# Rows of a down projection: from two raw blocks split in two parts to three raw blocks split product by product

## The chip, the core and the metric

The kernel runs on one core of one Trainium2 chip. Its time is the device time of one execution in microseconds (us). Before the change the median of 3 runs is 2338.86 us (2338.65 to 2340.06).

## What is computed

One layer of a decoder block on 1024 tokens of width 1024, all in float32: dilated attention in twelve heads and retention in four heads side by side, gated and projected, then a squared-ReLU MLP of width 4096. The change touches only the end of the MLP:

```python
xn2 = rmsnorm(x, norm2_g[l])
x = x + jnp.square(jax.nn.relu(xn2 @ w_up[l])) @ w_down[l]
```

Below, the result of the up projection after the squared ReLU is called h; it has 1024 rows of 4096 numbers. The down projection is `h @ w_down`.

## The kernel before

**Products of three terms.** TensorE multiplies float32 numbers in a rounded form, fp32r. So each factor is split into a high part (its rounding, written by ScalarE as a copy into an fp32r tile) and a low part (the residual, factor minus high part). A product is then three matmuls: high times high, high times low and low times high (`Pipe.group`, L218; its matmul is L223). Weights are split by `split` (L317): the copy at L318 on ScalarE, the residual at L319 on VectorE.

**Seven products instead of eight.** Both MLP projections use a Strassen-like scheme: a two-by-two block product is made from seven products N1 to N7 of sums of blocks. In the down projection a *unit* is one pair (c, t): c is one of 8 chunks of 512 inputs, t one of 4 groups of 128 rows of tokens, taken with the 128 rows 512 below. The 32 units run in the order of c, and of t within c. For one unit, each of the seven products takes one 128 x 256 block of rows (sums of parts of h, made during the up projection) and one 256 x 512 block of weights (sums of parts of w_down). A product is 6 matmuls: 2 blocks of 128 inputs, times three terms. A unit is 42 matmuls, the down projection 32 x 42 = 1344.

**Order on TensorE.** TensorE's order is that of the program. In the loop at the end, unit u runs N6, N5, N1 of unit u + 1, N7, N2 of unit u + 1, N3, N4. `down` (L1169) issues one product and reads its sum out of PSUM. N1 and N2 add up in bank a; N6, N7 and N4 in bank b, which ScalarE fills with minus N1 (L1187) before; N5 and N3 in bank d. After N2, N6, N5, N7, N3 and N4 the bank is added to Y in SBUF, by VectorE at L1195 (in chunk 0 some of these are plain copies by ScalarE, L1193). So N7 can start only when the sum after N6 has been read, N4 only after N7's has, N3 only after N5's has, and N2 only when ScalarE has copied N1's.

**Rows.** During the up projection `put_operand` (L1125) writes each sum of parts of h to the DRAM tensor `h_d`, laid out by chunk c and row group t, with the seven products of one unit side by side. `load_rows(u)` (L1142, DMA at L1146, issued on the SP queue) brings the block of unit u, 896 KB, into one of two raw places, which lie in the operand tile of N1 of the up projection (trace names xh and xl) once that is no longer needed. `split_rows` (L1148) splits it in two parts: the pair N1, N2 (one ScalarE copy of 512 columns at L1157, two GpSimd subtractions of 256 columns at L1160) and the other five (one copy of 1280 columns, five subtractions). The split pair goes to a pool of two, the split five to one of two places. `prepare(u)` (L1163), called at the start of the loop body, splits the five of unit u + 1, issues the load of unit u + 3 into the place that this frees, and splits the pair of unit u + 2.

**Weights.** The class `Weights` loads raw blocks of w_down (DMA at L176, SP queue too), forms the sums of blocks on VectorE (L153) and splits them. A weight buffer is free for the chunk after next when its product has run for t = 3 (`W.free`, L1199); the step that fills it is written at that place of the program. So a chunk has 7 splits and 4 sums for VectorE, written around its last unit and the first unit of the next chunk. N2's and N3's weights of odd chunks lie in two halves of one tile pair.

**Other adders to VectorE.** In chunks 2 to 5 every second unit adds one block of x to Y (L1253).

**Order on the other engines.** The order of the instructions on ScalarE, VectorE, GpSimd and the SP queue is chosen by a planner at build time, from the dependencies and from its own estimate of durations; at run time each of these engines takes its instructions strictly in that order, and one that waits holds up all behind it.

Of the kernel before, what the change touches and what calls it, by code (L numbers as in the profile page):

```python
# [10 lines left out]
F = mybir.dt.float32  # L11
R = mybir.dt.float32r
AF = mybir.ActivationFunctionType
OP = mybir.AluOpType
# [3 lines left out]
P = 128  # L18
# [188 lines left out]
class Pipe:  # L207
# [24 lines left out]
    def step(self, ps, terms, ends=None, first=True):  # L232
# [6 lines left out]
        def after(i):  # L239
# [11 lines left out]
           "N4": ("D", 0)}  # L251
DOWN = ("N1", "N2", "N6", "N5", "N7", "N3", "N4")
BANK = {"N1": "a", "N2": "a", "N6": "b", "N7": "b", "N4": "b", "N5": "d", "N3": "d"}
# [15 lines left out]
def hybrid_block(ctx: ExitStack, tc: tile.TileContext, a: dict, out: bass.AP):  # L269
# [25 lines left out]

    h_d = dram.tile([FF // 512, 4, P, 7, 2, P], F, name="h_d")
    y_d = dram.tile([S, D], F, name="y_d")
# [59 lines left out]
    for nb in range(2):  # L357
        for u in range(4):
            W.add(a["w_out"][nb, u], (4, 5, 2, 3)[u] if nb else (2, 3, 0, 1)[u])
    NU = FF // 256  # L360
    W.add_units("up", [a["w_up"][j] for j in range(NU)])
# [724 lines left out]
    with ExitStack() as ph:  # L1086
        up_pool, first_two, early, sumst = None, None, [], ExitStack()
        unit = {}

        def temps():  # L1090

            nonlocal up_pool
            if up_pool is None:
                assert pipe.slot > last_turn
                norm2.close()
                y0 = pool(sumst, "y0", 1)
                Y.update((r, y0.tile([P, D], F, name=f"Y{r}")) for r in (0, 4))
                nonlocal first_two
                first_two = pool(sumst, "rn", 2)
                up_pool = pool(ph, "p26", 2)  # L1100
            return up_pool
# [23 lines left out]
        def put_operand(j, name, x):  # L1125

            dst = h_d[j // 2, :, :, DOWN.index(name), j % 2]
            nc.sync.dma_start(dst.rearrange("t p q -> p t q"), x.rearrange("p (t q) -> p t q", q=P))
# [10 lines left out]
        raws = [x[:, :7 * 2 * P].bitcast(F) for x in flat("N1")]  # L1139
        row_places = [[x[:, :5 * 2 * P] for x in flat("N5")]]  # L1140

        def load_rows(u):  # L1142

            if u < len(units):
                c, t = units[u]
                nc.sync.dma_start(raws[u % 2], h_d[c, t].rearrange("p o k q -> p (o k q)"))  # L1146

        def split_rows(u, pair):  # L1148

            if u < len(units):  # L1150
                n = 2 if pair else 5
                if pair:
                    h, l = (first_two.tile([P, n * 2 * P], R, name=x) for x in ("rh", "rl"))
                else:
                    h, l = row_places[u % 2]
                src = raws[u % 2][:, :512] if pair else raws[u % 2][:, 512:]
                nc.scalar.activation(h, src, AF.Copy)  # L1157
                for i in range(n):
                    cs = slice(2 * P * i, 2 * P * i + 2 * P)
                    nc.gpsimd.tensor_tensor(l[:, cs], src[:, cs], h[:, cs].bitcast(F), op=OP.subtract)  # L1160
                rows[u, pair] = [x.rearrange("p (o k q) -> p o k q", o=n, k=2) for x in (h, l)]

        def prepare(u):  # L1163

            split_rows(u + 1, False)
            load_rows(u + 3)
            split_rows(u + 2, True)

        def down(u, name):  # L1169

            c, t = units[u]
            b = sums.setdefault(u, {})
            bank = BANK[name]
            fresh = bank not in b
            if fresh:
                b[bank] = mm.tile([P, 512], F, name="mm")
            o = DOWN.index(name)
            wh, wl = W["dn", c, name]
            xh, xl = rows[u, o < 2]
            o = o if o < 2 else o - 2  # L1180
            pipe.step(b[bank], [(xh[:, o, k], xl[:, o, k], wh[:, 512 * k:512 * k + 512], wl[:, 512 * k:512 * k + 512])
                                for k in range(2)], None, fresh)
# [23 lines left out]

        for j, name in strassen_order(NU):
            product("up", j, name, unit, OP7, temps, result)
            if j < NU - 1:
                continue  # L1210
            if name == "N1":
                load_rows(0)
                load_rows(1)
                split_rows(0, True)
            if name == "N2":
                weight_places("n2", name)
            if name == "N5":
                prepare(-1)
            if name == "N7":
                down(0, "N1")  # L1220
            if name == "N4":
                down(0, "N2")
            if name == "N3":
                weight_places("n3", name)
# [3 lines left out]
        Y.update((r, y1.tile([P, D], F, name=f"Y{r}")) for r in (1, 5))  # L1228
        row_places.append([y1.tile([P, 5 * 2 * P], R, name=f"r{x}1") for x in "hl"])
        W.places["y1a"] = [y1.tile([P, UW], R, name=f"y1a{x}") for x in "hl"]  # L1230
        Y.update((r, y1.tile([P, D], F, name=f"Y{r}")) for r in (3, 7, 2, 6))
        W.free(("place", "y1"))


    with ExitStack() as ph:
# [5 lines left out]
        for u in range(len(units)):  # L1241
            prepare(u)
            for name, later in (("N6", False), ("N5", False), ("N1", True), ("N7", False), ("N2", True),
# [110 lines left out]
```

## Time and profile before

| | |
|---|---|
| median of 3 runs | 2338.86 us (2338.65 to 2340.06) |
| profiled execution, its own time | 2336.11 us |
| its span, first to last instruction | 2334.3 us |
| TensorE matmuls busy over the span | 2254.4 us (97%) |
| VectorE / ScalarE / GpSimd busy | 1286.5 / 987.3 / 318.8 us |
| first product of the down projection | 1930.88 us after the span's start |
| last matmul starts | 2330.14 us |
| loads of rows `xh<-h_d`, `xl<-h_d` | 16 and 16, 896 KB each, 4.6 and 4.5 us to landing (median) |

Engines are named as in the profile: PE is TensorE's matmuls and PEld its weight loads, DVE is VectorE, ACT ScalarE, POOL GpSimd, SP the engine that issues the DMAs; a q after a name is the engine's queue. A row gives start and duration in us, engine, line, operation, output and inputs by the program's tile names; in brackets stands how long the engine was idle before it and what ended that. Matmuls overlap, so their pace is seen in the distance between their starts. Busy 97% is a mean over stages: in the up projection, which ends at the first row of the down projection above, TensorE is busy all the time, and in the down projection it is not.

### The profile page before, as it was taken

What the parts mean: (1) busy time and instruction counts of PE and PEld (TensorE: products, weight loads), DVE (VectorE), ACT (ScalarE), POOL (GpSimd) and SP (SyncE); (2) the same over time, 40 slices, a digit from 0 to 9 for tenths busy, and PEclk for the clock granted to TensorE, in tenths of its full rate; (3) what the DMA queues carried; (4) which work ended last, traced back from release to release, by engine and by line L of the source; (5) the groups of instructions that cost most, each with busy time, mean ns of one, the idle gap of its engine ahead of it and who ended that gap; (6) DMA issues with size and microseconds to landing.
All of it is one profiled execution on the core that took longest, in us unless ns stands there. A gap on an engine that the chain in (4) does not pass through costs nothing. (4 is left out here: it accounts for less than half of the span.)

```text
span 2334.3 us, 30051 instructions
## 1 busy us (share of the span) xinstructions
PE 2254.4 (97%) x10868; PEld 1925.9 (83%) x10868; DVE 1286.5 (55%) x2468; ACT 987.3 (42%) x2134; POOL 318.8 (14%) x372
## 2 busy tenths in 40 slices
PE   8999999999999999999999999999999999888888
PEld 7999999998888888888888778887788887666667
DVE  6345545456344445567777642537655566566553
ACT  6444444354343334345555431125555556332331
POOL 1111111110000000000000000000000005564553
PEclk9999999999999999999999999999999999889999
DMA  4213132332333333355333674543345566333323
GB/s 152 92 52 117 51 96 77 94 107 71 104 109 113 109 108 111 124 149 154 118 94 110 220 240 132 194 151 123 118 149 150 154 194 201 122 126 140 131 76 120
DMA packets 226855, 294.83 MB, mean 126 GB/s; under 512 B 14097, under 2 KB 157585, under 8 KB 226706
## 3 DMA queue, kind: packets, MB, share of 16 engines
q1 hardware_dynamic: 226706, 292.91, 39.3%
q8 instruction: 85, 1.39, 0.2%
q14 instruction: 64, 0.52, 0.1%
HBM read 200.48 MB, written 92.37 MB: 125 GB/s over the span
## 5 line engine op out<-in xcount | busy, mean ns | idle before, releaser
L319 DVE TENSOR_TENSOR wl<-raw,wh 128x1024 fp32r<-128x1024 f32 (+2 forms) x274 | 302.6, 1107 | 420.0 <-ACT wh L318 419.1
L223 PE MATMUL mm<-wh,xh 128*128 128x384 f32 (+1 forms) x1184 | 465.1, 393 | 0.7 <-DVE Y L1195 0.7
L223 PE MATMUL mm<-wh,xl 128*128 128x384 f32 (+1 forms) x1184 | 422.2, 357 | 2.2 <-DVE xl L319 2.2
L223 PE MATMUL mm<-wl,xh 128*128 128x384 f32 (+1 forms) x1184 | 421.0, 356 | 0.0
L318 ACT ACTIVATE wh<-raw 128x1024 fp32r<-128x1024 f32 (+2 forms) x274 | 260.4, 952 | 359.7 <-PE ms L223 105.0
L223 PE MATMUL mm<-xl,wh 128*128 128x512 f32 x848 | 309.7, 390 | 1.8 <-DVE xl L319 1.8
L223 PE MATMUL mm<-xh,wh 128*128 128x512 f32 x848 | 310.1, 390 | 0.0
L223 PE MATMUL mm<-xh,wl 128*128 128x512 f32 x720 | 280.4, 389 | 0.0
L223 PE MATMUL ms<-xh,wh 128*128 128x512 f32 x604 | 238.1, 394 | 3.1 <-DVE s L940 1.9
L223 PEld LDWEIGHTS mm<-wh,xl 128*128 128x128 f32 x1184 | 222.5, 188 | 20.8 <-DVE xl L319 3.1
L223 PEld LDWEIGHTS mm<-wh,xh 128*128 128x128 f32 x1184 | 223.7, 189 | 18.1 <-DVE Y L1195 1.6
L223 PEld LDWEIGHTS mm<-wl,xh 128*128 128x128 f32 x1184 | 224.5, 190 | 15.5 <-DVE wl L319 0.4
L223 PE MATMUL ms<-xh,wl 128*128 128x512 f32 x604 | 235.3, 390 | 0.0
L223 PE MATMUL ms<-xl,wh 128*128 128x512 f32 x604 | 235.2, 389 | 0.0
L223 PEld LDWEIGHTS mm<-xl,wh 128*128 128x128 f32 x848 | 159.5, 188 | 35.1 <-DVE xl L319 2.2
L223 PEld LDWEIGHTS mm<-xh,wh 128*128 128x128 f32 x848 | 159.5, 188 | 33.3 <-ACT ms L387 0.4
L223 PEld LDWEIGHTS mm<-xh,wl 128*128 128x128 f32 x720 | 135.4, 188 | 28.2
L223 PEld LDWEIGHTS ms<-xh,wh 128*128 128x128 f32 x604 | 113.5, 188 | 27.3 <-issue 2.3
L223 PEld LDWEIGHTS ms<-xh,wl 128*128 128x128 f32 x604 | 113.4, 188 | 23.7
L1160 POOL TENSOR_TENSOR rl<-xl,rh 128x256 fp32r<-128x256 f32 x112 | 119.3, 1094 | 99.7 <-ACT rh L1157 93.8
L223 PEld LDWEIGHTS ms<-xl,wh 128*128 128x128 f32 x604 | 113.5, 188 | 22.8 <-DVE xl L319 0.2
L852 POOL TENSOR_TENSOR st<-st,half 128x1 f32<-128x1 f32 x32 | 25.0, 780 | 766.2 <-DMA at<-acc_d 489.1
(284 smaller groups left out, 3611.2 us busy)
## 6 DMA issues: line engine op xcount, KB each, us to landing
raw<-in_w_att SPq DMA_DIRECT2D x48, 384.0 KB, 3.9
raw<-in_w_up SPq DMA_DIRECT2D x32, 512.0 KB, 3.9
h_d<-s SPq DMA_DIRECT2D x64, 256.0 KB, 4.4
raw<-in_w_down SPq DMA_DIRECT2D x32, 512.0 KB, 5.5
xh<-h_d SPq DMA_DIRECT2D x16, 896.0 KB, 4.6
xl<-h_d SPq DMA_DIRECT2D x16, 896.0 KB, 4.5
sg_d<-sg SPq DMA_DIRECT2D x32, 256.0 KB, 2.0
raw<-in_w_rqk_q SPq DMA_DIRECT2D x16, 512.0 KB, 3.5
```

The lines of the kernel that those rows point to most:

```text
L223: self.nc.tensor.matmul(ps, x, y, start=start, stop=stop, skip_group_check=not first)
L318: nc.scalar.activation(dst_h, src, AF.Copy)
L319: nc.vector.tensor_tensor(dst_l, src, dst_h.bitcast(F), op=OP.subtract)
L852: nc.gpsimd.tensor_tensor(st[:, 9:10], st[:, 8:9], half[:, 0:1], op=OP.pow)
L1160: nc.gpsimd.tensor_tensor(l[:, cs], src[:, cs], h[:, cs].bitcast(F), op=OP.subtract)
```

## The change

`h_d` is laid out by blocks in the order of use: block b holds N6, N5, N7, N3 and N4 of unit b - 1 and N1 and N2 of unit b. Block 0 has only N1 and N2 of unit 0, block 32 only the five of unit 31. There are three raw places; the third lies in the region `y1` where one of the places for the split five was. N1 and N2 of unit 0 are loaded by two small DMAs of their own. The split rows go to a ring of ten places of 256 columns, four in the pool `rn` and six in the operand tile pair of N5, which held the other place for the split five. `stream` lists all 224 products in the order of `down`. Before `down` issues product r it calls `part_rows`, which splits all products up to r + 8, each with one ScalarE copy and one GpSimd subtraction of 256 columns; so the split of product r + 8 is written into the place that product r - 2 used. When N4 of a block has been split, the load of the block three further on is issued, into the raw place just freed. `prepare` goes. The products, their order on TensorE, the weights and the evictions stay.

```diff
-DOWN = ("N1", "N2", "N6", "N5", "N7", "N3", "N4")
+
+DOWN = ("N6", "N5", "N7", "N3", "N4", "N1", "N2")
...
-    h_d = dram.tile([FF // 512, 4, P, 7, 2, P], F, name="h_d")
+    h_d = dram.tile([4 * (FF // 512) + 1, P, 7, 2, P], F, name="h_d")
...
-    NU = FF // 256
+    NU, RING = FF // 256, 10
...
-                nonlocal first_two
-                first_two = pool(sumst, "rn", 2)
+                first = pool(sumst, "rn", 1)
+                row_parts.extend(tuple(first.tile([P, 2 * P], R, name=f"r{x}{i}") for x in "hl") for i in range(4))
...
-            dst = h_d[j // 2, :, :, DOWN.index(name), j % 2]
+            b = 4 * (j // 2) + (name not in ("N1", "N2"))
+            dst = h_d[b:b + 4, :, DOWN.index(name), j % 2]
             nc.sync.dma_start(dst.rearrange("t p q -> p t q"), x.rearrange("p (t q) -> p t q", q=P))
...
         raws = [x[:, :7 * 2 * P].bitcast(F) for x in flat("N1")]
-        row_places = [[x[:, :5 * 2 * P] for x in flat("N5")]]
-
-        def load_rows(u):
-
-            if u < len(units):
-                c, t = units[u]
-                nc.sync.dma_start(raws[u % 2], h_d[c, t].rearrange("p o k q -> p (o k q)"))
-
-        def split_rows(u, pair):
...
-        def prepare(u):
-
-            split_rows(u + 1, False)
-            load_rows(u + 3)
-            split_rows(u + 2, True)
+        first_raw = {name: x[:, 7 * 2 * P:].bitcast(F) for name, x in zip(("N1", "N2"), flat("N1"))}
+
+        stream = [(0, "N1"), (0, "N2")]
+        for u in range(len(units)):
+            stream += [(u, "N6"), (u, "N5"), (u + 1, "N1"), (u, "N7"), (u + 1, "N2"), (u, "N3"), (u, "N4")]
+        stream = [(u, name) for u, name in stream if u < len(units)]
+        turns = dict(run=0, parted=0)
+
+        def load_rows(b):
+
+            if b == 0:
+                for o, name in enumerate(DOWN):
+                    if name in first_raw:
+                        nc.sync.dma_start(first_raw[name], h_d[b, :, o].rearrange("p k q -> p (k q)"))
+            elif b <= len(units):
+                n = 5 if b == len(units) else 7
+                nc.sync.dma_start(raws[(b - 1) % 3][:, :n * 2 * P], h_d[b, :, :n].rearrange("p o k q -> p (o k q)"))
+
+        def part_rows(upto):
+
+            while turns["parted"] < min(upto, len(stream)):
+                i = turns["parted"]
+                u, name = stream[i]
+                b = u + (name not in ("N1", "N2"))
+                o = DOWN.index(name)
+                src = raws[(b - 1) % 3][:, o * 2 * P:(o + 1) * 2 * P] if b else first_raw[name]
+                h, l = row_parts[i % RING]
                 nc.scalar.activation(h, src, AF.Copy)
...
+                nc.gpsimd.tensor_tensor(l, src, h.bitcast(F), op=OP.subtract)
+                rows[u, name] = [x.rearrange("p (k q) -> p k q", k=2) for x in (h, l)]
+                turns["parted"] += 1
+                if name == "N4":
+                    load_rows(b + 3)
 
         def down(u, name):
 
             c, t = units[u]
+            assert stream[turns["run"]] == (u, name)
+            part_rows(turns["run"] + RING - 1)
+            turns["run"] += 1
...
             if name == "N1":
-                load_rows(0)
-                load_rows(1)
-                split_rows(0, True)
+                for b in range(3):
+                    load_rows(b)
+                part_rows(4)
...
             if name == "N5":
-                prepare(-1)
+                row_parts.extend(tuple(x[:, 2 * P * i:2 * P * (i + 1)] for x in flat(name)) for i in range(6))
+                part_rows(9)
...
-        row_places.append([y1.tile([P, 5 * 2 * P], R, name=f"r{x}1") for x in "hl"])
+        raws.append(y1.tile([P, 7 * 2 * P], F, name="r2"))
...
         W.free(("place", "y1"))
+        load_rows(3)
...
         for u in range(len(units)):
-            prepare(u)
```

More of the change, by code (lines that the diff above doesn't have):

```diff
@@ L1086, in hybrid_block @@
     with ExitStack() as ph:
-        up_pool, first_two, early, sumst = None, None, [], ExitStack()
+        up_pool, early, sumst, row_parts = None, [], ExitStack(), []
         unit = {}
@@ L1139, in hybrid_block @@
         raws = [x[:, :7 * 2 * P].bitcast(F) for x in flat("N1")]
-        row_places = [[x[:, :5 * 2 * P] for x in flat("N5")]]
-        def load_rows(u):
-            if u < len(units):
-                c, t = units[u]
-                nc.sync.dma_start(raws[u % 2], h_d[c, t].rearrange("p o k q -> p (o k q)"))
-        def split_rows(u, pair):
[L1150 to L1161, printed above, removed]
@@ L1176, in down @@
                 b[bank] = mm.tile([P, 512], F, name="mm")
-            o = DOWN.index(name)
             wh, wl = W["dn", c, name]
-            xh, xl = rows[u, o < 2]
-            o = o if o < 2 else o - 2
-            pipe.step(b[bank], [(xh[:, o, k], xl[:, o, k], wh[:, 512 * k:512 * k + 512], wl[:, 512 * k:512 * k + 512])
+            xh, xl = rows[u, name]
+            pipe.step(b[bank], [(xh[:, k], xl[:, k], wh[:, 512 * k:512 * k + 512], wl[:, 512 * k:512 * k + 512])
                                 for k in range(2)], None, fresh)
```

## The prediction

> **What bounds the kernel now.** I read the busy time by stage first, to find where TensorE does not run. Each row below gives the stretch and its length, then the busy time (with the number of instructions) of TensorE's matmuls, its weight loads, VectorE, ScalarE and GpSimd, then the granted TensorE clock, the DMA share and GB/s. The first stretch holds the first products of the down projection among the last of the up projection; each stretch from 1970 to 2270 holds one change of weight chunk; the last one is the end.
>
> ```profile
> core 0 of [0], span 2334.3 us
> 1930.88:1953.16 22.28, 18.66 (x73) 14.32 (x71) 18.14 (x17) 14.84 (x22) 13.19 (x13) 0.92 0.67 214
> 1953.16:1970.00 16.84, 16.61 (x72) 13.44 (x72) 6.96 (x7) 9.63 (x15) 9.93 (x12) 1.00 0.77 269
> 1970.00:2017.00 47.00, 42.14 (x173) 34.02 (x174) 28.21 (x32) 20.79 (x28) 25.55 (x28) 0.93 0.35 123
> 2017.00:2068.00 51.00, 42.04 (x166) 33.52 (x164) 31.82 (x36) 15.39 (x19) 27.04 (x27) 0.90 0.37 134
> 2068.00:2119.00 51.00, 42.48 (x168) 33.89 (x168) 30.92 (x36) 16.08 (x20) 28.24 (x29) 0.90 0.35 124
> 2119.00:2170.00 51.00, 41.19 (x165) 32.54 (x165) 33.53 (x38) 14.91 (x18) 26.52 (x27) 0.90 0.40 142
> 2170.00:2223.00 53.00, 43.71 (x171) 34.67 (x170) 31.99 (x37) 17.54 (x21) 30.88 (x31) 0.90 0.31 112
> 2223.00:2270.00 47.00, 39.44 (x157) 30.79 (x156) 28.88 (x34) 14.12 (x17) 25.39 (x26) 0.93 0.20 68
> 2270.00:2330.50 60.50, 55.71 (x234) 44.31 (x232) 23.30 (x34) 10.98 (x14) 23.10 (x33) 0.97 0.34 115
> ```
>
> The chain of waits gives the price of a matmul that follows another without a pause:
>
> ```profile
> 2299.64 2.72 PE ms L223 x12
> ```
>
> That is 2.72 / 12 = 0.2267 us. A row's length less its matmuls times 0.2267 is what TensorE loses there: 22.28 - 73 x 0.2267 = 5.7 us at the entry, 0.5 in the next, 7.8, 13.4, 12.9, 13.6, 14.2 and 11.4 (together 73.3) in the six chunk changes, 7.5 at the end; 87 us in all. No engine is full there: VectorE has 31 to 34 of 51 us, GpSimd 27 to 28. So TensorE waits for an order of events, and the waits name it:
>
> ```profile
> PE ms L223 <- DVE Y L1195: 42.8, 10, 8.3
> PE mm L223 <- ACT ms L1187: 10.9, 8, 3.4
> ```
>
> TensorE waits for VectorE's additions into Y and for ScalarE's copies of N1's bank, never for the rows themselves. Who delayed those two engines? ScalarE's own waits over the same 400 us:
>
> ```profile
> ACT rh L1157 <- DMA xl<-h_d: 113.0, 15, 9.3
> ACT rh L1157 <- DMA xh<-h_d: 71.3, 12, 9.2
> ```
>
> ScalarE stands 184 us at the first split of a new block of rows, until that block has landed. One chunk change in order of time, ScalarE, then VectorE, then TensorE:
>
> ```profile
> 2025.49 0.63 ACT L1157 ACTIVATE rh<-xl 128x512 fp32r<-128x512 f32 x1 [8.96 <-DMA xl<-h_d]
> 2026.03 1.04 ACT L318 ACTIVATE xh<-raw 128x1024 fp32r<-128x1024 f32 x1
> 2027.11 1.59 DVE L319 TENSOR_TENSOR xl<-raw,xh 128x1024 fp32r<-128x1024 f32 x1 [6.78 <-ACT xh L318]
> 2029.21 1.27 DVE L1195 TENSOR_TENSOR Y<-Y,ms 128x512 f32<-128x512 f32 x2
> 2023.99 0.39 PE L223 MATMUL mm<-wh,rl 128*128 128x512 f32 x1
> 2030.54 0.80 PE L223 MATMUL ms<-w1ah,rh 128*128 128x512 f32 x1 [6.16 <-DVE Y L1195]
> 2031.13 0.63 PE L223 MATMUL ms<-w1al,rh 128*128 128x512 f32 x1
> 2031.56 0.63 PE L223 MATMUL ms<-w1ah,rl 128*128 128x512 f32 x1
> ```
>
> Read it backwards. N7 cannot add to its bank until N6 has been read out of it (two Y additions at 2029.21); these stand behind VectorE's residual of a weight block (2027.11), which waited 6.78 us for ScalarE's copy of it (2026.03), and that copy stood in ScalarE's queue behind a row split that waited 8.96 us for a DMA. After it TensorE's matmuls start 0.43 us apart instead of 0.23: the stall is paid a second time in the granted clock (0.90 to 0.93 in these rows). Why the rows are late is in the chain again, one turn of it:
>
> ```profile
> 2050.80 4.44 DMA xl<-h_d
> 2055.34 0.65 ACT rh L1157
> 2056.05 1.15 POOL rl L1160 x2
> 2057.44 3.53 POOL xl L1160 x5
> 2067.70 5.55 POOL rl L1160 x5
> ```
>
> With two raw places a block is loaded only when GpSimd has finished the five-product part of the block before it in that place, and ScalarE then waits out the landing: 4.44 + 0.65 + 1.15 + 3.53 and the hand-overs is 10.2 us (2050.80 to 2060.99), up to 2 us more when GpSimd takes 5.55. TensorE needs 42 x 0.2267 = 9.5 us a unit.
>
> **The change, part by part.** (1) Third raw block. The load of block b + 3 is issued once N4 of block b is split, eight products before N4 runs; the first split from block b + 3 comes 14 products later, at 6 x 0.2267 = 1.36 us each 19 us. A load takes 4.4 us; the queue that issues it has been held up for at most:
>
> ```profile
> SPq L1146 <- ACT xh L1157: 75.0, 13, 8.4
> ```
>
> 8.4 + 4.4 = 12.8 us is under 19, so the 184 us of ScalarE's waiting for rows go, and with them the wait ahead of the weight copies. Without that cover the old wait is back (rival D). The issues of the loads rise from 32 to 34 on a queue that mostly waits: nothing.
>
> (2) Splits product by product. ScalarE issues 7 copies of 256 columns a unit instead of one of 512 and one of 1280; GpSimd's subtractions stay 7 of 256 columns.
>
> ```profile
> L1157 ACT ACTIVATE rh<-xh x16: 613/634/636, 1906.9 to 2294.3; 128x512 fp32r<-128x512 f32 x16
> L1157 ACT ACTIVATE xh<-xh x16: 1254/1258/1283, 1927.7 to 2306.4; 128x1280 fp32r<-128x1280 f32 x16
> L1160 POOL TENSOR_TENSOR rl<-xl,rh x112: 722/744/1784, 1912.0 to 2318.2; 128x256 fp32r<-128x256 f32 x112
> ```
>
> The slope is (1.258 - 0.634) / 768 = 0.81 ns a column, so 256 columns cost about 0.43 us: 7 x 0.43 = 3.0 us against 1.9. The 1.1 us a unit lie in ScalarE's idle time (15 to 16 us busy of 51); with no idle time they would be 1.1 x 32 units = 35 us. GpSimd needs 7 x 0.74 = 5.2 us of each 9.5; at its worst 7 x 1.78 = 12.5 us, in a chunk change alone, where eight products in hand (10.9 us) cover the 3 us.
>
> (3) The new wait. The split of product r + 8 goes into the place that product r - 2 read, so ScalarE and GpSimd now wait for TensorE. Behind that wait on ScalarE stand weight copies and N1's copy, for which TensorE waits. It ends when r - 2 has run, and N1's copy belongs to a later product, so the wait cannot end later than the copy could start: between 0 and the 0.43 us of one split a unit; I take 0, as most copies have the idle ScalarE before them.
>
> (4) What then limits a chunk change. VectorE has 11 extra operations there (4 sums, 7 residuals), with both inputs in SBUF, and evictions between them. Its densest stretch:
>
> ```profile
> 2250.09 1.21 DVE L153 TENSOR_TENSOR raw<-raw,raw 128x1024 f32<-128x1024 f32 x1
> 2251.23 0.67 DVE L1195 TENSOR_TENSOR Y<-Y,ms 128x512 f32<-128x512 f32 x1
> 2251.83 1.21 DVE L153 TENSOR_TENSOR raw<-raw,raw 128x1024 f32<-128x1024 f32 x1
> 2252.96 1.76 DVE L319 TENSOR_TENSOR w1bl<-raw,w1bh 128x1024 fp32r<-128x1024 f32 x1
> 2254.65 0.67 DVE L1195 TENSOR_TENSOR Y<-Y,mm 128x512 f32<-128x512 f32 x1
> ```
>
> By their starts an eviction occupies 0.60 us, a sum or residual after it 1.14, and one that follows another such operation 1.69. TensorE brings six evictions in 9.5 us, one each 1.59 us; a pair on VectorE takes 1.74. Eleven pairs lag by 11 x 0.15 = 1.7 us, and some three contended ones add 3 x 0.55 = 1.7: 3.4 us of lag. An eviction of N6 or N7 may be late by two products less itself and a hand-over, 2.72 - 0.6 - 0.2 = 1.9 us. That leaves 1.5 us; with an addition of x between (it comes in half the units of the middle chunks) somewhat over 2. I take 2 us a change, 12 in all; the ends are 0 and, all eleven contended, 11 x 0.55 = 6.1 us each.
>
> [...]
>
> (5) Entry and end. At the entry ScalarE waits for a weight DMA, and VectorE has 18 of 22 us:
>
> ```profile
> 1935.43 6.10 DMA raw<-in_w_down
> 1941.61 1.07 ACT xh L318
> ```
>
> No row split is the cause, and just as many splits come there as before: I leave the 5.7 us (bounds 3 either way). At the end TensorE waits for N1's copy behind splits that wait for rows; weights no longer come: all 7.5 us go. Places and the layout of h_d change no instruction's size.
>
> The sum, against the profiled execution's own 2336.1 us (its span is 2334.3): 2336.1 - 73.3 + 12 - 7.5 = 2267.3. The median of the runs shown, 2338.86, lies 2.75 above it: **2270 us**, 2.9% faster.
>
> **Rivals.** A: VectorE takes over the chunk change. GpSimd's subtractions, no longer in bursts, meet all eleven operations: 6.1 us x 6 = 36 stay: 2336.1 - 73.3 + 36.6 - 7.5 + 2.75 = 2295. [...]
>
> B: nothing is left at the changes or the entry: 2336.1 - 86.5 + 2.75 = 2252. Against: VectorE's 18 of 22 us there.
>
> C, slower: the waits are kept for a whole tile, not for its slice. Six of the ten places are slices of one tile; then a product in one of them waits for the newest split into that tile, which waits for the product before. Places 6 to 9 would do so, 4 of 10 of 224 products, each with a copy, a subtraction and hand-overs, 0.43 + 0.74 + 0.3 = 1.5 us: 134 us on B's 2252 and the entry's 5.7, 2392. It is slower than now from about 0.9 us each. Against it: N3's and N2's weights of an odd chunk are two halves of one tile, and N3 of unit 6 ran at
>
> ```profile
> 2018.55 0.39 PE L223 MATMUL mm<-xh,xl 128*128 128x512 f32 x1
> ```
>
> although the write into the N2 half, issued before it in program order, came only at 2026.03 (above).
>
> D: the change doesn't do what it says. The issuing queue also carries weights and x; if the load of the third block is held up by over 15 us there, ScalarE waits as before: 2339. Longest hold-up so far 8.4.
>
> **How the numbers follow.** My forecast has 0.62 (its own range 2256 to 2286), A 0.18, B 0.10, D 0.04, C 0.06. The range is 2252 to 2302: B's value, and A's with its unknown. A measurement of this kernel can tell about 0.2%, 5 us, from no change; only D lies within it: faster 0.90, same 0.04, slower 0.06.
>
> **What would show it.** Right: ScalarE's waits for h_d near 0, its L1157 line with 224 copies near 0.43 us that wait for TensorE; no stall over 3 us on TensorE between 1970 and the end; granted clock near 1.00 there. A: VectorE over 0.85 busy at the changes, residuals at 1.7. Wrong altogether: TensorE waiting for L1160's subtractions (C), or ScalarE still for h_d (D).

## The result, and the profile after

The changed kernel takes 2268.34 us (median; 2267.41 to 2268.99), the kernel before, run beside it, 2339.46 us (2338.65 to 2342.3). The ratio is 0.9694, with a 95% interval of 0.9677 to 0.971: 3.1% faster. The forecast was 2270 us with a range of 2252 to 2302. The profiled execution took 2268.99 us, its span is 2267.2 us.

Busy time by stage of the changed kernel, with the columns of the prediction's first fence. The edges are the starts of the first matmuls behind the edges there.

```profile
1936.45:1959.57 23.12, 17.36 (x73) 13.09 (x71) 20.57 (x20) 15.26 (x27) 13.77 (x11) 0.96 0.73 231
1959.57:1979.16 19.59, 19.05 (x73) 15.22 (x73) 6.46 (x7) 11.97 (x24) 9.79 (x12) 0.87 0.73 263
1979.16:2019.55 40.39, 39.51 (x175) 32.40 (x174) 28.92 (x32) 23.17 (x46) 29.83 (x29) 1.00 0.43 144
2019.55:2057.63 38.08, 37.76 (x165) 30.62 (x164) 31.12 (x37) 19.46 (x38) 31.33 (x28) 1.00 0.52 180
2057.63:2096.30 38.67, 38.60 (x169) 31.11 (x167) 29.54 (x36) 19.87 (x40) 32.28 (x28) 1.00 0.47 164
2096.30:2135.39 39.09, 38.05 (x165) 30.55 (x164) 33.30 (x38) 19.18 (x39) 31.41 (x27) 1.00 0.53 183
2135.39:2174.51 39.12, 39.05 (x170) 31.49 (x169) 30.76 (x37) 20.33 (x40) 33.37 (x29) 1.00 0.45 154
2174.51:2210.56 36.05, 35.73 (x157) 28.94 (x155) 28.43 (x34) 19.02 (x37) 29.24 (x26) 1.00 0.30 103
2210.56:2263.15 52.59, 52.59 (x233) 43.36 (x231) 23.12 (x34) 14.64 (x34) 22.12 (x30) 1.00 0.29 100
```

Taken as the prediction took it, length less matmuls times 0.2267 us, 6.6 us are lost at the entry (5.7 before), 3.0 in the next stretch (0.5), 4.6 in the six chunk changes together (73.3 before) and nothing at the end (7.5). But a row also counts a matmul that only reaches across its edge, so the rows count some matmuls twice. With every matmul counted once, by its start, the changed kernel loses 6.8 us at the entry, 3.3 in the next stretch, 1.2, 0.9, 0.8, 1.9, 0.8 and 0.9 in the six changes (6.6 together) and nothing at the end. Over the same matmuls the kernel before loses 6.0, 1.6 and, in all behind, 81.8: its second row ends at 1970.00 us, 1.1 us ahead of the matmul that ends the second row here. So 17 us of 89 are left, and some 60% of them at the entry. The first product of the down projection starts 5.6 us later than in the profile of before (1936.45 against 1930.88). Together: +2.5 in the first 144 matmuls, -75.3 behind them and +5.6 by the later start are -67.2 us, against 2267.2 - 2334.3 = -67.1 us of span.

Whom TensorE waits for over the whole down projection in the changed kernel (total, times, longest, in us):

```profile
PE ms L223 <- DVE Y L1203: 5.0, 2, 4.3
PE mm L223 <- ACT ms L1195: 1.4, 2, 0.9
PE ms L223 <- ACT Y L1201: 1.3, 1, 1.3
PE mm L223 <- DVE Y L1203: 0.7, 3, 0.2
```

There were 42.8 us for VectorE and 10.9 for ScalarE's copies of N1. No subtraction of GpSimd (L1170) is in the list. ScalarE's own waits in the same kernel:

```profile
ACT xh L1169 <- PE mm L223: 43.6, 47, 1.5
ACT xh L1169 <- PE ms L223: 41.2, 41, 6.6
```

The 184 us of waits for rows that were landing are gone: the splits now wait for TensorE to leave a place of the ring, for 43.6 and 41.2 us in these two rows, the largest, and no row of the list names h_d. The new splits by their lines, with the least, the median and the longest duration in ns:

```profile
L1169 ACT ACTIVATE xh<-xh x47: 397/418/421, 1932.6 to 2242.8; 128x256 fp32r<-128x256 f32 x47
L1170 POOL TENSOR_TENSOR xl<-xl,xh x43: 727/739/2899, 1939.0 to 2244.6; 128x256 fp32r<-128x256 f32 x43
```

A copy of 256 columns takes 0.418 us; the estimate was 0.43.

**The entry.** The one long stall left is there. VectorE in the changed kernel, some of its operations in order of time:

```profile
1936.69 1.76 DVE L153 TENSOR_TENSOR raw<-raw,raw 128x1024 f32<-128x1024 f32 x1
1938.37 1.22 DVE L1121 TENSOR_TENSOR s<-q,s 128x512 f32<-128x512 f32 x1
1939.51 1.76 DVE L320 TENSOR_TENSOR wl<-raw,wh 128x1024 fp32r<-128x1024 f32 x1
1941.19 0.67 DVE L397 TENSOR_TENSOR u<-u,mm 128x512 f32<-128x512 f32 x1
...
1956.05 1.21 DVE L1121 TENSOR_TENSOR s<-q,s 128x512 f32<-128x512 f32 x1
1957.18 1.74 DVE L153 TENSOR_TENSOR raw<-raw,raw 128x1024 f32<-128x1024 f32 x1
1958.84 0.68 DVE L1203 TENSOR_TENSOR Y<-Y,ms 128x512 f32<-128x512 f32 x1
```

and TensorE at that place:

```profile
1954.92 0.39 PE L223 MATMUL mm<-wh,xl 128*128 128x512 f32 x1
1959.57 0.79 PE L223 MATMUL ms<-wh,xh 128*128 128x512 f32 x1 [4.27 <-DVE Y L1203]
1960.16 0.63 PE L223 MATMUL ms<-wl,xh 128*128 128x512 f32 x1
1960.59 0.63 PE L223 MATMUL ms<-wh,xl 128*128 128x512 f32 x1
```

N4 of unit 0 starts 4.65 us after the matmul before it, because the addition of N7's sum into Y (1958.84) stands last behind a row of weight and h operations. VectorE works without a pause from 1945.6 us on. After the stall twelve matmuls start 0.43 us apart, which makes 2.4 us of the second row's loss and its granted clock of 0.87.

Another piece is late from the start. The sum of weight blocks at 1936.69 and one of h at 1938.37 stand ahead of the up projection's residual (1939.51) and of the addition at 1941.19, for which ScalarE waits. Such sums stood there in the kernel before, too, but they were done when ScalarE's copy for the residual came, and the subtractions of that place, from 1929.04 us on, met little of them. Now they run beside five subtractions that fill the ring,

```profile
1933.13 5.91 POOL L1170 TENSOR_TENSOR xl<-xh 128x256 fp32r<-128x256 f32 x5 [14.53 <-ACT xh L1169]
```

and take 1.76 and 1.22 us, where they took 1.22 and 0.69 in the kernel before. ScalarE's wait in the changed kernel and, in the second fence, in the kernel before:

```profile
1941.90 0.63 ACT L1113 ACTIVATE u<-u 128x512 f32<-128x512 f32 x1 [3.14 <-DVE u L397]
```

```profile
1934.31 0.64 ACT L1112 ACTIVATE u<-u 128x512 f32<-128x512 f32 x1 [1.29 <-DVE u L396]
```

Counted from the first product, this piece starts at 5.45 us instead of 3.43, and what stands behind it is later by as much.

### The profile page after: what moved, and what is told of

Same layout as the page of the kernel before. It is cut to its first block, busy times and chain, and to the rows that moved or that the text cites. A ratio compares the mean times of both kernels' runs of the same rounds, so it can differ in the third digit from the quotient of the medians.

```text
span 2267.2 us, 30458 instructions
## 1 busy us (share of the span) xinstructions
PE 2233.0 (98%) x10868; PEld 1912.0 (84%) x10868; DVE 1285.7 (57%) x2468; ACT 1014.0 (45%) x2294; POOL 344.3 (15%) x372
## 5 line engine op out<-in xcount | busy, mean ns | idle before, releaser
L223 PE MATMUL mm<-wh,xh 128*128 128x384 f32 (+1 forms) x1226 | 482.0, 393 | 0.6 <-DVE Y L1203 0.5
L223 PE MATMUL mm<-wh,xl 128*128 128x384 f32 (+1 forms) x1226 | 438.8, 358 | 2.2 <-DVE xl L320 2.2
L223 PE MATMUL mm<-wl,xh 128*128 128x384 f32 (+1 forms) x1226 | 437.7, 357 | 0.0
L223 PEld LDWEIGHTS mm<-wh,xl 128*128 128x128 f32 x1226 | 230.9, 188 | 22.2 <-DVE xl L320 3.0
L223 PEld LDWEIGHTS mm<-wh,xh 128*128 128x128 f32 x1226 | 231.8, 189 | 20.0 <-DVE Y L1203 1.3
L223 PEld LDWEIGHTS mm<-wl,xh 128*128 128x128 f32 x1226 | 232.7, 190 | 16.6
L333 POOL TENSOR_TENSOR ssa<-ssa,half 128x2 f32<-128x2 f32 x96 | 66.5, 693 | 427.9 <-DVE ssa L332 411.2
```

What stands on the lines that cost most here:

```text
L223: self.nc.tensor.matmul(ps, x, y, start=start, stop=stop, skip_group_check=not first)
L333: nc.gpsimd.tensor_tensor(dst, dst, half[:, :w], op=OP.pow)
```

## The experiments

For every run the table gives the start of the first product, what TensorE loses in its first 72 matmuls, in the next 72 and in all the rest (each stretch less 72, 72 and 1223 times 0.2267 us, every matmul counted once by its start), the median and the ratio to the kernel before on the same chip. Profiles are single executions, medians are of four or five.

| kernel | first product | 72 | next 72 | rest | median us (lowest to highest) | ratio [95%] |
|---|---|---|---|---|---|---|
| before | 1930.9 | 6.0 | 1.6 | 81.8 | 2339.46 (2338.65 to 2342.3) | 1 |
| after | 1936.5 | 6.8 | 3.3 | 6.5 | 2268.34 (2267.41 to 2268.99) | 0.9694 [0.9677, 0.971] |
| ring_two_raws | 1931.3 | 7.1 | 1.0 | 6.5 | 2263.89 (2261.91 to 2264.92) | 0.9685 [0.9671, 0.9699] |
| three_raws_coarse | 1932.3 | 7.1 | 1.8 | 6.8 | 2260.81 (2258.95 to 2263.8) | 0.9674 [0.9659, 0.9689] |
| ring4 | 1932.1 | 4.7 | 2.2 | 8.4 | 2262.5 (2261.72 to 2263.27) | 0.968 [0.9666, 0.9695] |
| no_low_rows | 1932.5 | 3.2 | 1.2 | 2.2 | 2254.72 (2254.32 to 2255.11) | 0.9646 [0.963, 0.9662] |
| after_again | 1932.4 | 7.2 | 2.7 | 6.5 | 2264.78 (2263.88 to 2266.59) | 0.969 [0.9677, 0.9704] |
| pair_late | 1931.2 | 5.3 | 0.4 | 6.6 | 2259.38 (2258.62 to 2260.01) | 0.9666 [0.9653, 0.9679] |
| late_weights | 1931.7 | 4.4 | 1.6 | 6.5 | 2261.0 (2258.72 to 2262.32) | 0.9672 [0.9659, 0.9685] |
| ramp | 1932.4 | 6.7 | 2.3 | 6.7 | 2264.17 (2263.38 to 2266.99) | 0.9689 [0.9676, 0.9702] |
| pair_late_again | 1931.0 | 5.2 | 0.4 | 6.6 | 2259.83 (2259.1 to 2264.59) | 0.967 [0.9656, 0.9684] |
| pair_late_weights | 1934.8 | 2.1 | 1.9 | 7.1 | 2258.23 (2256.36 to 2261.71) | 0.9656 [0.9643, 0.967] |

ring_two_raws, three_raws_coarse, ring4 and no_low_rows ran side by side on one chip (the kernel before: 2336.45 us); after_again, pair_late, late_weights and ramp on a second (2337.57); the last two on a third (2337.7).

**Which part carries the gain?** First the fine ring without the third block (an edit of the changed kernel):

```diff
-                nc.sync.dma_start(raws[(b - 1) % 3][:, :n * 2 * P], h_d[b, :, :n].rearrange("p o k q -> p (o k q)"))
+                nc.sync.dma_start(raws[(b - 1) % 2][:, :n * 2 * P], h_d[b, :, :n].rearrange("p o k q -> p (o k q)"))
...
-                src = raws[(b - 1) % 3][:, o * 2 * P:(o + 1) * 2 * P] if b else first_raw[name]
+                src = raws[(b - 1) % 2][:, o * 2 * P:(o + 1) * 2 * P] if b else first_raw[name]
...
-                    load_rows(b + 3)
+                    load_rows(b + 2)
...
-        raws.append(y1.tile([P, 7 * 2 * P], F, name="r2"))
...
-        load_rows(3)
```

> The changed kernel with the third raw block taken away: ring of ten places, splits product by product eight ahead, but two raw places, so that the block two further on is loaded when N4 of a block has been split. Theory (the gain is that ScalarE no longer stands at a row split until a DMA lands; what counts is how long before its first split a block is loaded): here the load has 7 products, 7 x 1.36 = 9.5 us, against a landing of 4.4 us, so ScalarE's waits for h_d stay under 20 us in all and the time is 2268 to 2276. Rival (the third block is needed): the wait comes back at each block, ScalarE waits over 100 us for h_d and the time is above 2300.

Then the third block without the fine ring (an edit of the kernel before; so that it fits, the second place for a pair lies in the rest of N5's tile, and the pool of x blocks has one buffer):

```diff
-                first_two = pool(sumst, "rn", 2)
+                first_two = pool(sumst, "rn", 1)
+                pair_places.append([first_two.tile([P, 4 * P], R, name=x) for x in ("rh", "rl")])
...
-                nc.sync.dma_start(raws[u % 2], h_d[c, t].rearrange("p o k q -> p (o k q)"))
+                nc.sync.dma_start(raws[u % 3], h_d[c, t].rearrange("p o k q -> p (o k q)"))
...
-            load_rows(u + 3)
+            load_rows(u + 4)
...
+        raws.append(y1.tile([P, 7 * 2 * P], F, name="r2"))
...
+        load_rows(2)
...
-        px = pool(ph, "px7", 2)
+        px = pool(ph, "px7", 1)
```

> The kernel before with a third raw block and nothing else of the change: splits still in two parts (512 and 1280 columns), the load of unit u + 4 in place of u + 3 when the five products of unit u + 1 are split. To make room one of the two places for the pair lies in the rest of the operand tile of N5, and x for the end is loaded into one place in place of two. Theory (only ScalarE's wait for the landing matters): a load now has a unit more, 9.5 us and more, so the waits for h_d fall from 184 us to under 20 and the time is 2268 to 2285, as in the changed kernel. Rival (the fine splits bring the gain, since long copies and five subtractions in a row hold up the engines): it stays above 2310.

And the ring with four places instead of ten, so that a split runs two products ahead:

```diff
-    NU, RING = FF // 256, 10
+    NU, RING = FF // 256, 4
...
-                part_rows(9)
+                part_rows(3)
```

> The changed kernel with a ring of four places in place of ten, so two products ahead in place of eight; the six places in the operand tile of N5 are not used. Theory (the depth of the ring is cover for the changes of chunk alone, where a subtraction takes up to 1.78 us of 1.36): between the split's start and its use lie three products, 4.1 us, for 0.43 + 0.74 to 1.78 us and ScalarE's weight copies of 1.05 us, so TensorE waits for rows now and then at the changes of chunk, 1 to 4 us each: 2270 to 2295. Rival (eight ahead is not needed at all): 2262 to 2270, the entry being shorter since GpSimd splits less ahead there.

The stretch from the 144th matmul to the last one, one fence for each of the three, in that order:

```profile
1972.09:2255.87 283.78, 281.19 (x1224) 228.41 (x1223) 204.82 (x245) 135.93 (x270) 209.18 (x195) 1.00 0.44 148
```

```profile
1973.83:2257.87 284.04, 281.15 (x1224) 228.49 (x1223) 205.12 (x245) 113.75 (x130) 189.11 (x194) 1.00 0.41 148
```

```profile
1971.61:2257.25 285.64, 281.42 (x1225) 228.50 (x1223) 205.28 (x245) 138.18 (x276) 213.98 (x201) 1.00 0.43 147
```

The kernel before spent 359.05 us on the same matmuls, the changed one 283.76. Each part alone gives the whole of it. With two raw places and the ring, ScalarE waits for no h_d at all, and the time, 2263.89 us, lies a little below what the theory expected of that kernel. With three places and coarse splits ScalarE waits for h_d once, here from its waits:

```profile
ACT rh L1159 <- DMA r<-h_d: 0.4, 1, 0.4
```

That is the theory's case again, with a time that is also below its interval: the rival, that the fine splits are needed, fell. A ring of four costs 1.9 us of these 75, as the rival had it, by which the depth is not needed; TensorE does wait for GpSimd there:

```profile
PE mm L223 <- POOL rl L1170: 1.4, 2, 0.7
```

So two raw places alone were not what held the kernel before, as the prediction had said, nor was the size of a split, nor is the depth needed. What closed the loop in the kernel before?

**What GpSimd takes from VectorE.** The changed kernel without the subtractions:

```diff
-                nc.gpsimd.tensor_tensor(l, src, h.bitcast(F), op=OP.subtract)
-                rows[u, name] = [x.rearrange("p (k q) -> p k q", k=2) for x in (h, l)]
+                rows[u, name] = [x.rearrange("p (k q) -> p k q", k=2) for x in (h, h)]
```

> The changed kernel without GpSimd's subtractions of the row splits: the low part of the rows is left out and the high part stands in its place, so the numbers are not the reference's. It shows what VectorE and GpSimd cost each other. Theory (at the entry VectorE is full and its operations run against the ring's first subtractions, 1.2 and 1.7 us instead of 0.7 and 1.2; at the changes of chunk they cost next to nothing): the entry's stall of 4.65 us goes and little else, 2258 to 2264. Rival A of the prediction in a small form (the subtractions cost at every change): the stalls after 1970 go too, 2252 to 2257. If neither: 2266 to 2270.

It measured 2254.72 us, in the interval of rival A in a small form and below that of the theory. Across chips the ratios have to be compared (the kernel before took 2336.45 us on one, 2337.57 on the other): 0.9646 against after_again's 0.969 is 0.0044 x 2337 = 10 us, and the table's rows put 4.0 of them at the first 72 matmuls, 1.5 at the next and 4.3 in the rest, 0.7 for each chunk change. VectorE at the entry without GpSimd:

```profile
1949.58 0.68 DVE L1121 TENSOR_TENSOR s<-q,s 128x512 f32<-128x512 f32 x1
1950.18 1.21 DVE L153 TENSOR_TENSOR raw<-raw,raw 128x1024 f32<-128x1024 f32 x1
```

The same sum of h took 1.21 us at 1956.05 in the changed kernel, the same kind of sum of weights 1.74 at 1957.18. So the subtractions do lengthen VectorE's operations, as rival A has it, but all that they cost is 10 us, not the 36 at the changes that it was priced at.

**The order in ScalarE's queue.** ScalarE in the kernel before, over two units:

```profile
2055.34 0.64 ACT L1157 ACTIVATE rh<-xl 128x512 fp32r<-128x512 f32 x1 [7.49 <-DMA xl<-h_d]
2055.88 1.26 ACT L1157 ACTIVATE xh<-xh 128x1280 fp32r<-128x1280 f32 x1
...
2065.58 0.63 ACT L1157 ACTIVATE rh<-xh 128x512 fp32r<-128x512 f32 x1 [7.85 <-DMA xh<-h_d]
2066.12 1.26 ACT L1157 ACTIVATE rh<-xl 128x1280 fp32r<-128x1280 f32 x1
```

The first row is the pair of the newest block, in raw place xl, and waits until that block has landed. The five of the block before it, in xh, stand behind it, though their rows have lain there for a unit. Only when they are done is xh free for the next load, whose pair then stands ahead of the five in xl. So each landing waits for the one before: landing, pair, five, load, landing. That is the 10.2 us of the prediction's chain, and the order has a part in it beside the number of places. In the program `prepare` writes the five first; in ScalarE's queue the planner has put the pair ahead of them. To test the order, the kernel before with its two raw places and coarse splits, in which the pair is written later, after N2 (unit u + 1's) has run; the pair's pool then needs one buffer, not two, and the pair comes after the five:

```diff
-                first_two = pool(sumst, "rn", 2)
+                first_two = pool(sumst, "rn", 1)
...
             load_rows(u + 3)
-            split_rows(u + 2, True)
...
                 down(0, "N2")
+                split_rows(1, True)
...
                     down(u + later, name)
+                if name == "N2":
+                    split_rows(u + 2, True)
```

> The kernel before with its two raw blocks and its two coarse splits; only the pair (N1 and N2 of unit u + 2) is split later: it has one place in place of two, and its split is written after N2 of unit u + 1 in the loop, not at the head of unit u. Theory (before, the two splits stood in ScalarE's queue in an order that closed a loop: the pair of the newest block, still on its way, stood ahead of the five of the block before, and only that five frees the place for the next load, so landing, pair, five and the next load came in a row, 10.2 to 12.2 us a unit against TensorE's 9.5): the pair can now not stand ahead of the five, the load has about half a unit to land, ScalarE's waits for h_d fall from 184 us to under 40 and the time is 2260 to 2285. Rival (two raw blocks with coarse splits are too few in any order): waits for h_d stay above 100 us and the time above 2310.

ScalarE in this kernel, over two units:

```profile
2051.17 1.27 ACT L1157 ACTIVATE xh<-xh 128x1280 fp32r<-128x1280 f32 x1 [1.00 <-PE ms L223]
...
2058.11 0.63 ACT L1157 ACTIVATE rh<-xl 128x512 fp32r<-128x512 f32 x1 [0.21 <-PE mm L223]
...
2060.69 1.28 ACT L1157 ACTIVATE rh<-xl 128x1280 fp32r<-128x1280 f32 x1
...
2068.21 0.63 ACT L1157 ACTIVATE rh<-xh 128x512 fp32r<-128x512 f32 x1 [0.83 <-PE mm L223]
```

The five of xh are split at 2051.17, 7 us before the pair of xl, and no split waits for a row any more: the wait is for TensorE. Its stretch from the 144th matmul on:

```profile
1969.51:2253.32 283.81, 281.08 (x1224) 228.45 (x1223) 204.02 (x245) 114.52 (x131) 192.09 (x196) 1.00 0.42 149
```

That is the whole gain again: 283.81 us where the kernel before has 359.05 and the changed one 283.76. And at 2259.38 us it is 5.4 us faster than the changed kernel beside it (2264.78), with 1.9 us less at the first 72 matmuls, 2.3 less at the next, and 1.2 for the earlier start. In the ring the splits follow the order of use, so there, too, a five no longer stands behind the landing of the block after it. Three places leave the order as it was. In three_raws_coarse the pair of a block, in xl, still runs ahead of the five of the block before, in xh:

```profile
2052.95 0.63 ACT L1159 ACTIVATE xh<-xl 128x512 fp32r<-128x512 f32 x1 [1.08 <-PE mm L223]
...
2055.61 1.28 ACT L1159 ACTIVATE xh<-xh 128x1280 fp32r<-128x1280 f32 x1 [1.08 <-PE ms L223]
```

But the load of that block was issued at 2041.48, 11.5 us ahead, so the pair does not wait for it. The loop thus needs both, two places and the pair ahead of the five, and without either of them it is open. The kernels of the table in which it is open lose at most 8.4 us after the entry, the one in which it is closed 81.8. A ring in which the newest pair is put ahead again was not tried.

**The entry.** after_again is the changed kernel once more. Its expectation:

> The changed kernel once more, as the mark for the others of this call and as a second profile of it. Its order of instructions is that of the kernel before up to about 1905 us, so the 5 us by which its first profile was later there should be a difference between executions, not the change's: first product of the down projection at 1931 to 1936 us, loss behind it 15 to 18 us, 2263 to 2269.

```profile
1932.39:1955.96 23.57, 17.36 (x73) 13.09 (x71) 21.02 (x20) 15.14 (x27) 14.47 (x11) 0.93 0.75 235
```

The losses are those of the first profile, but the first product starts at 1932.39 us, not at 1936.45. So 4.1 of the 5.6 us by which it came late there belong to that execution and not to the change.

late_weights moves the first fill of the place y1 behind unit 0, in the changed kernel:

```diff
-        W.free(("place", "y1"))
         load_rows(3)
...
+            if u == 0:
+                W.free(("place", "y1"))
```

> The changed kernel with the weights of chunk 1 split later: the places for them in y1 are told free only after unit 0, not before the loop. Theory (the entry's 7 to 10 us are VectorE's: chunk 1's sums and residuals stand between the last sums of the up projection and the first evictions, though chunk 1 begins only 30 us later): the entry's stalls of 1.7 and 4.65 us become under 2 in all, with their slow clock, and VectorE's idle time of 6 us in unit 1 is used: 4 to 8 us faster than the changed kernel of this call. Rival (the work only moves and stalls TensorE in unit 1 or 2): within 2 us of it.

It gained 3.8 us beside after_again, just under the 4 to 8 that were expected, and its first row says where:

```profile
1931.67:1952.35 20.68, 17.41 (x73) 13.09 (x72) 16.85 (x17) 15.47 (x27) 12.19 (x11) 1.00 0.80 257
```

VectorE has 17 operations in the first stretch instead of 20, and the stretch is 2.9 us shorter. The long stall and its slow clock are gone (granted 1.00), but in the first 144 matmuls four stalls of 1.1 to 1.7 us between the starts of two matmuls are left, where under 2 us in all were expected. ramp instead lets the splits run ahead step by step at the start:

```diff
-            part_rows(turns["run"] + RING - 1)
+            part_rows(turns["run"] + min(RING - 1, 4 + turns["run"] // 2))
...
-                part_rows(9)
+                part_rows(4)
```

> The changed kernel, whose ring is filled slowly: at the entry four products are split ahead, and one more for each two products that run, up to eight. Theory (GpSimd's burst at the entry makes VectorE's operations there longer, 1.2 and 1.7 us instead of 0.7 and 1.2): the burst is spread over the first ten products, the stall of 4.65 us shrinks by 1 to 3 us: 2 to 4 us faster than the changed kernel of this call. Rival (the burst has to be paid in any case, or the planner puts the splits where it likes): within 1.5 us of it.

2264.17 against 2264.78 us, with ranges that overlap: the rival's case, no difference. But the planner left the burst where it was: in both kernels GpSimd has eleven subtractions in the first stretch, and the five that fill the ring start at 1928.54 us here and at 1928.97 in after_again. So whether a burst that is spread would help stays open. That the burst costs something is seen in ring4, which does without these five: with the same order on VectorE ScalarE's wait of 3.14 us for the addition is 0.6 us there, in no_low_rows 0.5, in late_weights still 3.2. So two things are late at the entry, VectorE's work on the weights of chunk 1 and operations that GpSimd's subtractions lengthen.

**Both edits together** on the kernel before (the later pair, and the later first fill of y1), beside pair_late once more:

> The kernel before with the two edits that paid by themselves: one place for the pair, split after N2 of the unit before, and the weights of chunk 1 split only after unit 0. Theory (the two work at different places: the loop of the rows in units 1 to 31, VectorE's and ScalarE's queues at the entry): the entry's loss of 5.7 us falls to 2 to 4, the rest stays at about 6.5, so 1 to 4 us faster than the late pair alone, 2255 to 2259. Rival (the late pair's entry waits for ScalarE's copy into Y behind a weight DMA, which the later weights leave in place): within 1 us of the late pair alone.

> The late pair once more, as the mark for the other kernel of this call: 2257 to 2261 us, and ScalarE without waits for h_d.

Its median is 2258.23 us, 1.6 us below pair_late's 2259.83 with ranges that overlap: not shown to be better. Its loss in the first 144 matmuls is 4.0 us against 5.6, but its profiled execution, with 2261.71 us the longest of its five, has a first product that comes 3.8 us later. By their ratios both lie 0.2 to 0.4% below the changed kernel (0.9656 to 0.967 against 0.969 to 0.9694); side by side on one chip this was measured for pair_late alone, with ranges that do not overlap.

## Why the prediction was right, and which steps were not

**What bounds the kernel: right.** TensorE's stalls at the chunk changes went through VectorE and the weight copies back to a row split that waited for a DMA; with that wait gone, the rest of the down projection goes from 359.05 to 283.76 us.

**Step "With two raw places a block is loaded only when ...": half of the cause.** The chain of waits that it quoted is right, and holds the pair (0.65 and 1.15 us) between the landing and the five. But the loop was read as a matter of places alone. It needs the order, too: the pair of a block in flight ahead of the five of a block that is there. pair_late keeps two places and changes the order, three_raws_coarse keeps the order and has three places, and of the 184 us of waits at most 0.4 are left over the same stretch in either; ring_two_raws, with two places, has none. Part (1), "the 184 us ... go", came true, but the third block that it gives the credit to is one of three ways, and is not needed with the ring, nor the ring with the third block.

**(2) right.** 0.418 us a copy for 0.43; GpSimd's median subtraction is still 0.74 us, and TensorE waited for none.

**(3) right.** ScalarE's waits for TensorE are many (84.8 us in the two rows above) and cost almost nothing: N1's copies make TensorE wait 1.4 us in all, for 32 units, 0.04 us each.

**(4) too high: 12 us forecast, 6.6 measured.** The sum that failed is "3.4 us of lag, 1.9 us of room". In the changed kernel VectorE alternates at a chunk change as foreseen:

```profile
2071.05 0.67 DVE L1203 TENSOR_TENSOR Y<-Y,mm 128x512 f32<-128x512 f32 x1
2071.65 1.21 DVE L320 TENSOR_TENSOR wl<-raw,wh 128x1024 fp32r<-128x1024 f32 x1
2072.78 0.67 DVE L1203 TENSOR_TENSOR Y<-Y,ms 128x512 f32<-128x512 f32 x1
```

A pair starts 1.73 us after the one before (2071.05 to 2072.78), as the 1.74 said, and the residual between takes 1.21 and not 1.76. But TensorE loses 0.8 to 1.9 us a change, below the 2 us and inside its ends of 0 and 6.1. no_low_rows puts 0.7 us of each change down to GpSimd; which of the other terms was too large, the runs don't separate. The granted clock stays at 1.00 there.

**(5) the entry's loss rose, the end's went.** "I leave the 5.7 us": over the same 144 matmuls 7.6 us became 10.1. The 2.5 us more are inside the 3 that were allowed, but the reason given, that just as many splits come there as before, looked at their number and not at what runs beside them. GpSimd's subtractions now run beside VectorE's sums and residuals and lengthen them (at the entry a sum of weights to 1.76 us from 1.22, one of h to 1.22 from 0.69), and VectorE got 20 operations in the first stretch, against 17. no_low_rows and late_weights show both, 5.5 and 3.9 us at the first 144 matmuls. The end lost nothing, as forecast.

**The sum.** The forecast of the profiled execution was 2267.3 us, measured 2268.99. From the 145th matmul on, the change gave 75.3 us where 73.3 - 12 + 7.5 = 68.8 were forecast, 6.5 more; the first 144 took 2.5 more, and the later start, which the sum did not have, 5.6, of which 4.1 belong to that execution. Together these make 1.6 of the 1.7. The 2.75 us from the profiled execution to the median did not repeat either: here the median is 0.65 below it. That the total came within 2 us of 2270 is thus in part luck: errors of 2.5 to 6.5 us cancelled.

**The rivals.** A holds in that the subtractions lengthen VectorE's operations, but they cost 4.3 us at the changes and not 36. In the kernel before, from 1900 us on, no residual or sum of weights without a subtraction beside it took over 1.23 us, and one beside subtractions took up to 1.80 (2184.20); the additions at L1195 took at most 0.69 either way. In no_low_rows three residuals in a row start 1.14 and 1.13 us apart (1956.70, 1957.84 and 1958.97), where the prediction read 1.69. B (2252 us) fell by what is left at the entry and the changes, and by the later start; the kernel without GpSimd's subtractions comes nearest, at 2254.72. C fell: with ten places no wait of TensorE is for a split (the rows of its waits name neither L1169 nor L1170), so no product waited for the newest split into its tile. D fell: the queue that issues the loads stood for up to 10.5 us at a load whose raw place was not free yet (8.4 before), and no split waited for rows:

```profile
SPq L1158 <- POOL xl L1170: 117.8, 18, 10.5
```

## What to carry to other kernels

When an engine waits long for a transfer, look first at what stands behind the waiting instruction in its queue: if the work that frees the buffer for the next transfer is there, the two form a closed loop, and, where they can change places, swapping the two instructions can be worth as much as another buffer and a finer split (here 283.81 us behind the entry against 283.76). A chain of waits shows the loop but not which link to cut, so try the cheapest cut by itself. Where a planner orders the other engines, a change in one stage can also move work in the stages beside it (here VectorE's 20 operations in the first stretch for 17): count the instructions by stage in both profiles.

## What the runs showed of the hardware

**Beside VectorE's sums and residuals a subtraction took up to 2.90 us.** The longest subtraction of 256 columns on GpSimd was 2.16 us in the kernel before (1.78 in the group that the prediction shows); the row of L1170 above has one of 2.90 us. With no operation of VectorE beside it but additions at L1195 (L1203 in the changed kernel) none took over 0.77 us before and 0.74 after. In pair_late five of them took 8.41 us, 1.68 each, where five took 3.53 us beside additions at L1195 alone (2057.44 in the kernel before); in the kernel before, too, five took up to 7.89 us (at 2042.88), more than the 5.55 that the prediction had read:

```profile
2062.04 8.41 POOL L1160 TENSOR_TENSOR rl<-xl,rh 128x256 fp32r<-128x256 f32 x5 [0.36 <-ACT rh L1157]
```

It cost nothing there: TensorE waited for none.

**After stalls of 2.18 and 2.44 us TensorE's matmuls came slower, after 2.25 and 2.68 us not.** A stall is counted here from one start to the next. In the changed kernel the stall of 4.65 us was followed by matmuls 0.43 us apart. In the kernel before, one of 2.44 us was too, and one of 2.18 (the restart at 2308.23):

```profile
2094.30 0.39 PE L223 MATMUL mm<-y1ah,rl 128*128 128x512 f32 x1
2096.74 0.50 PE L223 MATMUL ms<-w1ah,xh 128*128 128x512 f32 x1 [2.05 <-DVE Y L1195]
...
2097.68 0.63 PE L223 MATMUL ms<-w1ah,xh 128*128 128x512 f32 x1
```

Within a microsecond of the restart a matmul takes 0.63 us instead of 0.39. Others were not: after 1.69 us at 1950.50 in the changed kernel, 2.25 us at 1954.74 in ring_two_raws and 2.68 us in three_raws_coarse the next matmuls start 0.23 us apart (granted clock 1.00 from 1954.74 to 1972.09 in ring_two_raws and from 1932.33 to 1955.72 in three_raws_coarse). The last of them:

```profile
1947.37 0.50 PE L223 MATMUL ms<-xh 128*128 128x512 f32 x1 [2.29 <-ACT Y L1195]
```

In the down projection of the kernel before and of the changed one no stall up to 2.01 us was followed by the slow pace, and every one from 3.19 us on was (nine before, one after). For those between, the length of the stall alone does not decide; what else does, no run here settles.

**The start of a stage differs between executions of one kernel.** The same kernel's first product of the down projection came at 1936.45 us in one profile and at 1932.39 in another, with medians of 2268.34 and 2264.78 us and ratios to the kernel before of 0.9694 and 0.969. Single profiles of two kernels can so differ by 4 us for no reason of theirs, which is as much as the edits at the entry are worth.
